# Low parts of the weights: a negated copy on ScalarE and an adding transfer in place of GpSimd's subtraction

## The chip, the cores and the metric

The kernel runs on one core of a Trainium2 chip. The metric is the device time of one execution in microseconds; the median of three runs of the kernel before is 2039.91 us (2033.06 to 2041.58).

## The reference

Two layers of a trunk, run for two groups of rows that share all weights: a prompt of 512 rows and a sample of 32 rows with cached state. One layer:

```
h = rmsnorm(x);  P = h @ w_in                      # 1024 -> 7688 columns, shared out to all branches
A: glu -> causal depthwise conv (31) -> LayerNorm -> silu -> @ w_conv_out
B: retention, 8 heads, rotary q/k, chunks -> GroupNorm * silu gate -> @ w_ret_out
C: forgetting attention, 8 heads, QK-norm, causal, cumulative log-forget bias -> @ w_fox_out
x = x + (sig(gA)*A + sig(gB)*B + sig(gC)*C) @ w_out
x = x + (gelu(causal dwconv3(h2 @ W_a)) * (h2 @ W_b)) @ W_down,   h2 = rmsnorm(x)
```

All inputs are fp32. The outputs are both groups' rows and their new states.

## The kernel before

Both groups are laid side by side as 544 columns (32 + 512), channels on the partitions. Every projection is a product of a weight block of 128 x 128 with the activations, in two halves of 272 columns. To come close to fp32 with fp32r matmuls, weights and activations are each split into a high part, which is the value rounded to fp32r, and a low part, which is value minus high part. One block takes three matmuls per half: high x high, high x low and low x high (`gemm`, L305).

The weights come in units of 8 blocks, a tile of 128 x 1024 (512 KB). There are 146 units per layer, 292 in all, packed in the order of use. The class `Stream` brings them in. `load_part` (L195) has SP issue the transfer of a unit into a `raw` tile, of which there are two. `split_part` has ScalarE write the high part into `hi` (L203), and then GpSimd subtract `hi` from `raw` into `lo` (L204). There are three `hi` and three `lo` buffers. The first two units are split on VectorE by the setup code (L415 to L421), the other 290 by `split`.

The order of work is the program's order, and every engine works its own queue in that order. Each projection is a `slot` (L311): it takes the next unit, then `ahead` splits the unit after the next and loads the one two further on, then a piece of side work runs (`tick`), then the gemm of 48 matmuls, then its eviction (`done`). So a unit's split is written down two gemms ahead of its use, and its `hi` waits until the gemm three units back has given up the buffer. GpSimd's other work is small or late: a few copies and memsets, the rotary products (L813, L815), two splits of the attention's keys and queries (L605, L609), partial sums of the convolution (L490).

Side work is woven between the gemms: the 31-tap convolution on VectorE (L483, 27 steps for each of four channel blocks and layer), the attention (L701 and L712 for the sample, L751 to L784 for the prompt, with exp and copies such as L765 on ScalarE), the retention (L858 to L920), the norms (rsqrt L343 to L353). R-scaled evictions are L394; in the FFN, L1138 to L1151 evict, convolve three taps and apply gelu. L444 evicts the first two gemms of all.

Of the kernel before, what the change touches and what calls it, by code (L numbers as in the profile page):

```python
# [11 lines left out]
F32 = mybir.dt.float32  # L12
F32R = mybir.dt.float32r
AF = mybir.ActivationFunctionType
ALU = mybir.AluOpType
# [96 lines left out]
def trunk(ctx, tc, x_in, wpack, wff, consts, params, s_conv, s_ret, s_cache, s_clf, s_ffn,  # L112
          y_out, o_conv, o_ret, o_fk, o_fv, o_lf, o_ffn):
    nc = tc.nc
    PS = bass.MemoryType.PSUM
    mm = nc.tensor.matmul
    act = nc.scalar.activation
    vtt = nc.vector.tensor_tensor
    stt = nc.vector.scalar_tensor_tensor
    gtt = nc.gpsimd.tensor_tensor  # L120
# [61 lines left out]
    class Stream:  # L182
# [14 lines left out]
        def split_part(self, u, i, sub, n=2):  # L197
            if i == 0:
                self.hl[u] = [upool.tile([P, UW], F32R, tag=t, name=t, bufs=3) for t in ("hi", "lo")]
                self.ns += 1  # L200
            hi, lo = self.hl[u]
            sl = slice(i * UW // n, (i + 1) * UW // n)
            act(hi[:, sl], self.raw[u][:, sl], AF.Copy)  # L203
            sub(lo[:, sl], self.raw[u][:, sl], hi[:, sl].bitcast(F32), op=ALU.subtract)  # L204
            if i == n - 1:
                self.raw.pop(u)

# [4 lines left out]
        def split(self, upto):  # L212
            while self.ns <= min(upto, DEPTH * NU - 1):
                self.load(self.ns)
                self.split_part(self.ns, 0, gtt, 1)

        def take(self):
            u = self.at
# [1078 lines left out]
```

## Time and profile before

| | us |
|---|---|
| median of 3 runs | 2039.91 |
| the profiled execution | 2039.84 |
| its span, first to last instruction | 2038.1 |
| TensorE busy | 1969.1 |
| VectorE busy | 1225.7 |
| GpSimd busy | 900.7 |
| ScalarE busy | 788.2 |
| transfers, mean share of the 16 engines | 29.2% |

PE is TensorE's matmul, PEld its weight load, DVE is VectorE, ACT is ScalarE, POOL is GpSimd and SP is SyncE, which issues all transfers here. L305 is line 305 of the kernel. Matmuls are pipelined: a duration of 0.29 us goes with a new matmul every 0.125 us. An arrow `<-` in brackets names what ended the idle time before an instruction. In the tables of stretches the columns are the bounds and the length of the stretch, the busy us of PE, PEld, DVE, ACT and POOL with their instructions in brackets, the granted TensorE clock as a share of 2.4 GHz, the busy share of the 16 transfer engines, and GB/s.

### The profile page before, as it was taken

Reading aid. Unit: us, or ns where it says so; the run is one execution under the profiler, and the core shown is the slowest. Engines: PE = TensorE matmul, PEld = TensorE weight load, DVE = VectorE, ACT = ScalarE, POOL = GpSimd, SP = SyncE. Lnnn points to the kernel's source line nnn. Section 1 sums busy time; section 2 is a strip of 40 time slices with the busy share of each in tenths; the row PEclk is TensorE's granted clock in tenths of the full one; section 3 lists DMA queues with packets and bytes.
Section 4 is the critical chain, followed back from the end, with each engine's and each line's share of the span. In section 5 each row is a group of like instructions: output and inputs, shape, how many; then the busy total and the mean of one; then the engine's idle time right before and its main releaser. Section 6 shows DMA issues by size and latency. Waiting matters only on the chain.

```text
span 2038.1 us, 37239 instructions
## 1 busy us (share of the span) xinstructions
PE 1969.1 (97%) x15768; PEld 1913.6 (94%) x15768; DVE 1225.7 (60%) x1641; ACT 788.2 (39%) x1172; POOL 900.7 (44%) x580
## 2 busy tenths in 40 slices
PE   8999998999999999999999888989999999999999
PEld 7987888999999999999999877889999999999999
DVE  5587989666355660466326979995653656505640
ACT  4354552264334331233335445523452343313331
POOL 4463544244444444444444645432444344444442
PEclk9999999999999999999999999999999999999999
DMA  5353312122232222222433622112223322222232
GB/s 200 92 174 108 94 48 76 58 73 87 90 127 90 87 89 89 86 91 87 131 112 105 182 85 88 53 56 67 81 83 101 120 83 85 93 83 94 83 105 76
DMA packets 69075, 194.22 MB, mean 95 GB/s; under 512 B 14012, under 2 KB 15660, under 8 KB 68524
## 3 DMA queue, kind: packets, MB, share of 16 engines
q1 hardware_dynamic: 68908, 191.84, 29.2%
q8 instruction: 124, 2.03, 0.4%
q14 instruction: 43, 0.35, 0.1%
HBM read 169.07 MB, written 9.89 MB: 88 GB/s over the span
## 4 chain that ended last, share of the span: by engine, by line
PE 71%; DVE 22%; ACT 3%; issue 3%; DMA 1%; POOL 0%; SPq 0%; DVEq 0%; ACTq 0%; POOLq 0%
PE acc L305 68%; DVE w L483 10%; DVE w L756 1%; DVE q L324 1%; ACT hi L203 1%; DVE w L755 1%; DVE w L394 1%; DVE mn L687 1%; DVE w L353 1%; PE s L752 0%; DVE w L352 0%; DVE q L843 0%; ACT q L323 0%; DVE w L873 0%; DVE q L1019 0%
## 5 line engine op out<-in xcount | busy, mean ns | idle before, releaser
L305 PE MATMUL acc<-q,hi 128*128 128x272 f32 x9344 | 1789.6, 291 | 23.3 <-ACT q L323 9.0
L305 PEld LDWEIGHTS acc<-q,hi 128*128 128x128 f32 x9344 | 1475.3, 189 | 42.8 <-issue 9.4
L305 PE MATMUL acc<-q,lo 128*128 128x272 f32 x4672 | 1349.6, 289 | 0.0
L204 POOL TENSOR_TENSOR lo<-raw,hi 128x1024 fp32r<-128x1024 f32 x290 | 714.4, 2464 | 849.4 <-ACT hi L203 811.6
L305 PEld LDWEIGHTS acc<-q,lo 128*128 128x128 f32 x4672 | 883.0, 189 | 0.0
L203 ACT ACTIVATE hi<-raw 128x1024 fp32r<-128x1024 f32 (+1 forms) x293 | 309.4, 1056 | 735.4 <-PE acc L305 601.7
L483 DVE SCALAR_TENSOR_TENSOR w<-w,par 128x574 f32<-128x574 f32 x208 | 247.4, 1190 | 3.5
L1179 DVE TENSOR_TENSOR q<-acc,q 128x544 f32<-128x544 f32 x32 | 23.2, 725 | 208.9 <-PE acc L305 208.9
L1146 DVE SCALAR_TENSOR_TENSOR w<-w,par 128x546 f32<-128x546 f32 x44 | 93.6, 2128 | 42.9 <-ACT w L1145 42.9
L394 DVE TENSOR_TENSOR w<-acc,R 128x544 f32<-128x544 f32 x78 | 56.1, 720 | 95.5 <-PE acc L305 95.4
L321 DVE TENSOR_TENSOR q<-w,q 128x544 fp32r<-128x544 f32 x44 | 92.4, 2099 | 31.9 <-ACT q L320 31.9
L1148 ACT ACTIVATE w<-w 128x546 f32<-128x546 f32 x44 | 29.1, 662 | 129.7 <-DVE w L1147 129.6
L689 ACT ACTIVATE w<-w,mn 128x128 f32<-128x128 f32 (+4 forms) x68 | 38.0, 559 | 81.4 <-DVE mn L687 79.1
L324 DVE SCALAR_TENSOR_TENSOR q<-q,par 128x544 fp32r<-128x544 f32 x24 | 49.0, 2042 | 22.4 <-ACT q L323 22.4
L1141 POOL COPY fb<-w 128x2 f32<-128x2 f32 x44 | 8.1, 185 | 117.8 <-DVE w L1138 117.8
L1138 DVE TENSOR_TENSOR w<-acc,R 128x32 f32<-128x32 f32 x44 | 8.4, 192 | 83.2 <-PE acc L305 83.0
L813 POOL TENSOR_TENSOR w<-w,cst 128x544 f32<-128x544 f32 x16 | 26.2, 1641 | 65.7 <-DMA w<-q 59.7
L692 ACT ACTIVATE w<-w,rs 128x128 f32<-128x128 f32 (+4 forms) x68 | 37.9, 557 | 32.1 <-DVE rs L691 31.7
L490 POOL TENSOR_TENSOR w<-w 128x574 f32<-128x574 f32 x24 | 43.4, 1809 | 12.8 <-ACT w L486 11.2
L330 DVE TENSOR_TENSOR wr<-w,wr 128x544 fp32r<-128x544 f32 x24 | 27.2, 1133 | 33.3 <-ACT wr L329 33.3
L352 DVE SCALAR_TENSOR_TENSOR w<-s,w 128x272 f32<-128x272 f32 (+1 forms) x60 | 23.7, 436 | 38.1 <-ACT w L349 38.1
L1018 DVE SCALAR_TENSOR_TENSOR w<-w,acc 128x544 f32<-128x544 f32 x32 | 23.0, 720 | 37.3 <-PE acc L305 37.0
(207 smaller groups left out, 1563.2 us busy)
## 6 DMA issues: line engine op xcount, KB each, us to landing
raw<-in_wpack_dram SPq DMA_DIRECT2D x291, 512.0 KB, 3.3
q<-wr SPq DMA_DIRECT2D x64, 128.0 KB, 2.4
w<-in_x_dram SPq DMA_DIRECT2D x16, 272.0 KB, 4.2
w<-q SPq DMA_DIRECT2D x64, 68.0 KB, 3.0
ck<-cscr SPq DMA_DIRECT2D x16, 256.0 KB, 3.4
out_dram<-wr SPq DMA_DIRECT2D x8, 272.0 KB, 2.4
out_dram<-w SPq DMA_DIRECT2D x8, 272.0 KB, 2.6
xn<-q SPq DMA_DIRECT2D x8, 272.0 KB, 4.0
```

The source lines that it names most:

```text
L203: act(hi[:, sl], self.raw[u][:, sl], AF.Copy)
L204: sub(lo[:, sl], self.raw[u][:, sl], hi[:, sl].bitcast(F32), op=ALU.subtract)
L305: mm(acc[:, h, :HN], w, half(x, h), start=(i == 0 and j == 0), stop=(i == n - 1 and j == len(passes) - 1))
L321: vtt(lo, src, hi.bitcast(F32), op=ALU.subtract)
L324: stt(lo, src, scale, hi.bitcast(F32), op0=ALU.mult, op1=ALU.subtract)
L394: vtt(two(out), acc, two(self.R), op=ALU.mult)
L483: stt(c, u[:, k : k + CO], pcol(w + k), c, op0=ALU.mult, op1=ALU.add)
L490: gtt(p, p, t, op=ALU.add)
L689: act(L[:, :n], L[:, :n], AF.Exp, scale=-1.0, bias=mn, accum_out=sm)
L692: act(L[:, :n], L[:, :n], AF.Copy, scale=rs)
L1146: stt(c, a[:, 1 : 1 + FO], pcol(w + 1), c, op0=ALU.mult, op1=ALU.add)
L1148: act(c, c, AF.Gelu)
```

## The change

For the 290 units that `split` prepares, `lo` is no longer computed by GpSimd. ScalarE writes the negative of `hi` into `lo`, and GpSimd issues a transfer from HBM that adds the unit's weights onto `lo`. The weights are thereby read from HBM twice, once into `raw` for `hi`, and once into the sum. The first two units keep VectorE's subtraction.

```diff
             hi, lo = self.hl[u]
             sl = slice(i * UW // n, (i + 1) * UW // n)
             act(hi[:, sl], self.raw[u][:, sl], AF.Copy)
-            sub(lo[:, sl], self.raw[u][:, sl], hi[:, sl].bitcast(F32), op=ALU.subtract)
+            if sub is None:
+
+                act(lo[:, sl], hi[:, sl].bitcast(F32), AF.Copy, scale=-1.0)
+                nc.gpsimd.dma_start(lo[:, sl], wpack[u][:, sl], accum_op=ALU.add)
+            else:
+                sub(lo[:, sl], self.raw[u][:, sl], hi[:, sl].bitcast(F32), op=ALU.subtract)
             if i == n - 1:
                 self.raw.pop(u)
...
         def split(self, upto):
             while self.ns <= min(upto, DEPTH * NU - 1):
                 self.load(self.ns)
-                self.split_part(self.ns, 0, gtt, 1)
+                self.split_part(self.ns, 0, None, 1)
```

## Rows read from the trace of the kernel before

**Rows 1.** The page: busy us (share of span) and instructions; chain shares by engine.
```profile
PE 1969.1 (97%) x15768; PEld 1913.6 (94%) x15768; DVE 1225.7 (60%) x1641; ACT 788.2 (39%) x1172; POOL 900.7 (44%) x580
...
PE 71%; DVE 22%; ACT 3%; issue 3%; DMA 1%; POOL 0%; SPq 0%; DVEq 0%; ACTq 0%; POOLq 0%
```

**Rows 2.** Table of stretches: from:to, length, busy us (instructions), clock, DMA share, GB/s.
```profile
102.00:408.00 306.00, 284.32 (x2344) 260.53 (x2344) 256.75 (x372) 135.18 (x263) 139.91 (x73) 0.97 0.30 93
408.00:1019.00 611.00, 607.86 (x4831) 605.98 (x4830) 313.78 (x376) 225.36 (x278) 269.95 (x193) 1.00 0.29 94
1121.00:1427.00 306.00, 281.18 (x2338) 256.44 (x2337) 255.73 (x361) 134.11 (x262) 136.56 (x69) 0.98 0.29 89
1427.00:1987.00 560.00, 556.86 (x4412) 554.98 (x4411) 292.62 (x349) 201.27 (x245) 248.16 (x182) 1.00 0.28 92
```

**Rows 3.** Table of waits, TensorE: us in total, times, longest us.
```profile
PE s L701 <- DVE w L712: 10.2, 2, 5.2
...
PE t L763 <- ACT w L765: 8.7, 7, 2.3
PE acc L305 <- DVE w L394: 8.5, 6, 2.5
PE s L631 <- DVE w L352: 7.3, 2, 3.7
...
PE o L892 <- DVE w L873: 5.2, 2, 2.6
```

**Rows 4.** Chain of waits, 102 to 200 us: start us, us, what.
```profile
159.57 0.83 DVE w L483
...
162.64 2.83 DVE w L483
```

**Rows 5.** Timeline, 155 to 171 us: start us, us, instruction, count [idle before <- releaser].
```profile
162.31 2.53 POOL L204 TENSOR_TENSOR lo<-raw,hi 128x1024 fp32r<-128x1024 f32 x1 [4.24 <-ACT hi L203]
...
169.98 1.07 PE L701 MATMUL s<-q,w 64*32 64x256 f32 x8 [4.98 <-DVE w L712]
```

**Rows 6.** Groups by line and shape: count | busy us, mean ns | idle before, releasers.
```profile
L204 POOL TENSOR_TENSOR lo<-raw,hi 128x1024 fp32r<-128x1024 f32 x290 | 714.4, 2464 | 849.4 <-ACT hi L203 811.6 <-DMA raw<-in_wpack_dram 20.7 <-PE t L763 14.8
L203 ACT ACTIVATE hi<-raw 128x1024 fp32r<-128x1024 f32 x291 | 308.2, 1059 | 735.0 <-PE acc L305 601.7 <-issue 122.8 <-DMA raw<-in_wpack_dram 6.3
L483 DVE SCALAR_TENSOR_TENSOR w<-w,par 128x574 f32<-128x574 f32 x208 | 247.4, 1190 | 3.5
L1146 DVE SCALAR_TENSOR_TENSOR w<-w,par 128x546 f32<-128x546 f32 x44 | 93.6, 2128 | 42.9 <-ACT w L1145 42.9
...
L1147 DVE SCALAR_TENSOR_TENSOR w<-w,par 128x546 f32<-128x546 f32 x44 | 34.7, 789 | 1.6
```

**Rows 7.** Table of stretches, L204 alone: DVE and POOL busy, clock, DMA share, GB/s.
```profile
102.00:408.00 306.00, 0.00 (x0) 83.12 (x33) 0.97 0.30 93
```

**Rows 8.** Timeline of a steady stretch in the FFN.
```profile
704.56 1.06 ACT L203 ACTIVATE hi<-raw 128x1024 fp32r<-128x1024 f32 x1 [4.03 <-PE acc L305]
...
705.70 2.40 POOL L204 TENSOR_TENSOR lo<-raw,hi 128x1024 fp32r<-128x1024 f32 x1 [0.62 <-ACT hi L203]
706.47 2.21 DVE L1146 SCALAR_TENSOR_TENSOR w<-w,par 128x546 f32<-128x546 f32 x1 [0.97 <-ACT w L1145]
...
716.59 1.06 ACT L203 ACTIVATE hi<-raw 128x1024 fp32r<-128x1024 f32 x1 [4.04 <-PE acc L305]
```

**Rows 9.** DMA issues: engine, operation, count, KB each, median us from issue to landing.
```profile
raw<-in_wpack_dram SPq DMA_DIRECT2D x291, 512.0 KB, 3.3
...
q<-in_s_cache_dram SPq DMA_DIRECT2D x2, 1024.0 KB, 7.0
```

**Rows 10.** Table of stretches, a steady one in the FFN's down projection.
```profile
764.30:815.20 50.90, 50.90 (x409) 50.90 (x408) 4.35 (x6) 9.54 (x9) 20.43 (x9) 1.00 0.27 89
```

**Rows 11.** Timeline of the start.
```profile
20.42 1.05 ACT L203 ACTIVATE hi<-raw 128x1024 fp32r<-128x1024 f32 x1
...
25.90 0.63 ACT L444 ACTIVATE w<-acc 128x544 f32<-128x544 f32 x1 [0.52 <-PE acc L305]
```

## The prediction

> **What bounds the kernel now.** The page's first part comes first: TensorE is busy in 97% of the span [rows 1]. A change that leaves the matmuls alone can win back only its idle time, 2038.1 - 1969.1 = 69.0 us. The table of stretches shows where that lies: 306.0 - 284.3 = 21.7 us in the first layer's attention and convolution part (102 to 408 us), 306.0 - 281.2 = 24.8 us in the second's (1121 to 1427), 3.1 us in each of the two long stretches with gates, FFN and down projection (408 to 1019, 1427 to 1987) [rows 2], and the other 16 us at the start, between the layers and at the end. So the two attention parts decide, with 46.5 us; I call them A and B. In them VectorE is busy 84% of the time (256.8 of 306), and the granted clock is 0.97 and 0.98 rather than 1.00: short times at the lower level (1.2 of 2.4 GHz), worth some 9 + 6 = 15 us.
>
> The table of waits names what TensorE idled for: 10.2 us for L712, 8.5 for L394, 7.3 for L352, 5.2 for L873, all on VectorE, 31 us together, and 8.7 us at 7 places for ScalarE's copy L765 [rows 3]; by their lines these belong to A and B. The chain of waits ahead of the longest one is a file of L483 convolution steps on VectorE: most take 0.83 us, some 2.83 [rows 4]. The timeline says which: the one of 2.83 us, at 162.64, runs beside GpSimd's subtraction L204 (162.31 to 164.84), and TensorE's 5 us of waiting at L701 end at the close of that file [rows 5].
>
> **What goes: the subtraction on GpSimd.** 290 instructions of 2464 ns, 714 us [rows 6]. GpSimd is not on the path (0% of the chain [rows 1]), so their own time is worth nothing. What counts is what they do to VectorE. L1146 and L1147 have the same form and 546 columns, yet take 2128 and 789 ns [rows 6]; L1146 is the one that falls beside L204 [rows 8]. L483 takes 1190 ns on average and 0.83 us when left alone [rows 4, 6]: 0.36 x 208 = 75 us too much; it is the convolution, which runs in A and B. GpSimd's own work in A is 139.9 us, of which L204 has 83.1, that is 59% [rows 2, 7]. I give the subtraction 59% of the 75: 45 us of VectorE's time released. L1146 would also shrink, by 1.3 us x 44, but it stands in the FFN, in the stretches where TensorE is busy 99% of the time [rows 2]: worth nothing.
>
> How much of the 45 us reaches the end? The 31 us of waits named for VectorE are the ceiling. In the file before L701 a stretched step costs 2.0 us of a 5.0 us wait [rows 4, 5]; other steps are stretched by GpSimd work that stays. Between none and all I take 60% of 31, by the 59%: **-19 us**. Fewer idle times leave fewer times at the lower clock: a quarter of 15, **-4 us**. Bounds: 0, and -31 - 15 = -46.
>
> **What comes: a second pass on ScalarE.** 290 x 1.06 us = 307 us [rows 6], 33 of them or 35 us in A [rows 7], on top of ScalarE's 135 of 306 [rows 2], so it becomes no bound. The new pass stands right behind `hi` in a queue that keeps its order, and what is queued behind it (tanh, exp, the copies L765, the splits) starts up to 1.06 us later. In the FFN that is covered: L1145 starts 1.06 us later, and the 2.2 us L1146 behind it should fall to about 0.8 [rows 6, 8]. In A and B, TensorE waits for L765 at 7 places [rows 3]; at most 7 x 1.06 = +7 us, at least 0, I take the middle, **+4 us**.
>
> **What comes: the adding transfer.** It waits for ScalarE's second pass, and GpSimd's copies, rotary products and klo splits queue behind it, as they queue today behind L204, which waits 812 us in all for `hi` [rows 6]. The matmuls now wait for its landing. The budget, from a steady part: `hi` runs from 704.56 to 705.62, when a gemm has just ended; its unit is used two gemms later, and the second one's end is seen at 716.59, 12.03 us on (6.0 us a gemm) [rows 8]. From the end of `hi` that is 10.9 us; less 1.06 for the second pass and 0.1 for the handover, 9.7 us are left for issue and landing. Today L204 ends at 708.10 [rows 8], with 8.4 us to spare.
>
> The trace has no transfer issued by GpSimd and none that adds, so both are bounded. Issue: between nothing and the 2.4 us of the arithmetic that it replaces; I take 1.0, nearer to the lower end since it works on no tile. Landing: a plain 512 KB weight load lands in 3.3 us, and 1024 KB, as much as target and source together, in 7.0 us [rows 9]. The engine time of a plain one: 0.27 of the 16 engines over 6.0 us [rows 10], 1.6 us. Adding must read the target too, so I take twice that, 3.2 us, and a landing of 3.3 + 1.6 + 0.6 = 5.5 us, between the two rows. Issue and landing make 6.5 us of 9.7: hidden in steady state. The engines would be at 0.27 x 3 = 0.81. The upper end for the adding is four times a plain load, 0.27 x 5 = 1.35, and that is not hidden (rival 2).
>
> The Trainium skill, in "Collectives: The Full Stack" (The bandwidth ceiling), says that a reducing transfer runs at half a copy's rate because it reads two sources, and not because the adder costs time. By it the 0.81 holds and the sum stands; no row here shows it.
>
> Not hidden is the start: unit 2's `hi` runs from 20.42 to 21.47, and its first gemm follows the one that L444 evicts at 25.90 [rows 11]. With 21.5 + 1.1 + 6.5 = 29.1 us the weights are about **+3 us** late, once; with the bounds 0 + 3.3 and 2.4 + 7.0 it is 0 to +6.
>
> **What moves.** The raw buffer comes free when `hi` ends, not when L204 ends, some 2.5 us sooner; SP, whose next weight load stands waiting for that buffer, gets on sooner, and with it the transfers queued behind. The next raw weights are early anyway (`hi` mostly waits for TensorE, 601.7 us [rows 6]), so I count it as 0.
>
> **The sum.** -19 - 4 + 4 + 3 = -16 us on the profiled execution's own 2039.84 us (span 2038.1), which is the median of the runs to 0.1 us: **2024 us**. Its bounds: -46 + 0 + 0 = -46 (1994) and 0 + 7 + 6 = +13 (2053); its own likely range is 1998 to 2035.
>
> **Rivals.** *1. No change, about 2037.* The issue holds VectorE up just as the subtraction did, for as long as it lasts, and A and B are paced by ScalarE. With 1.0 of 2.4 us held, 58% of the 19 us stay: -11 - 2 + 7 + 3 = -3 us. For it: the exp and tanh chains alternate between the two engines. Against: ScalarE is busy in only 44% of A. The Trainium skill, "SBUF — State Buffer" (Who interferes with whom), says that VectorE with two inputs in SBUF collides with GpSimd instructions that read SBUF, not with ones that only write. By that an issue would release VectorE entirely and this rival loses its first half; the rows show the collision with a reading instruction, none with a writing one. Chance 0.20.
>
> *2. Slower: the transfer engines become the bound.* It decides where adding costs three times a plain load's engine time: 0.27 x 4 = 1.08, and a gemm of 6.0 us waits for 6.5 us of transfers. In the two steady stretches, 611 + 560 = 1171 us [rows 2], 8% are 94 us: about 2135 us. At four times, 1.35, it is +410 us: 2450. Landing over 8.7 us behind a 1.0 us issue does the same by latency: TensorE waits in every unit. For it: each of 290 weight tiles passes, and 27% is used already. Against: reading HBM and reading SBUF are both plain work, and twice leaves 19% free. Chance 0.25.
>
> *3. Slightly slower, about 2053.* The upper bounds +7 and +6 with no relief on VectorE, because GpSimd's rotary and klo work, which stays, meets the convolution as often as L204 did. Chance 0.05.
>
> **From this to the numbers.** Forecast 0.50, rivals 0.20, 0.25, 0.05. A difference of 0.5% (10 us) is about what a measurement can tell from none. Faster 0.50 (forecast), same 0.20 (rival 1), slower 0.30 (rivals 2 and 3). About 0.05 lie under 1998, and 0.15 above 2140 (rival 2 beyond threefold cost), so the range is 1998 to 2140; rival 2 sets its upper end.
>
> **What would show it.** Right: L483 near 0.9 to 1.0 us on average and L1146 near 0.8; TensorE's idle time in A and B down from 46 to about 25 us; no wait of L305 for a transfer into `lo` after unit 3; a transfer share near 0.8 in the FFN. Wrong: waits of L305 for `lo` in every unit, a transfer share at 1.0, a landing over 8.7 us (rival 2); L483 still at 1.1 us or more (rival 1); more waits for L765 and later `hi` (rivals 1 and 3).

## The result: 2007 us, 1.5% faster, twice the forecast's gain

The kernel after takes 2006.89 us (median, 2003.81 to 2014.27) where the kernel before took 2039.67: a ratio of 0.9847 [0.9829, 0.9865], 32.8 us less. The forecast was 16 us less. The profiled execution took 2007.52 us, its span is 2005.8. Line numbers behind the diff are 5 higher than before: L305 is now L310, L483 is L488, L1146 is L1151.

The page of the kernel after: busy time by engine, then the DMA queues (GpSimd's is q0), then the chain's shares.

```profile
PE 1964.9 (98%) x15768; PEld 1911.1 (95%) x15768; DVE 943.4 (47%) x1641; ACT 1065.2 (53%) x1462; POOL 425.9 (21%) x580
...
q0 software_dynamic: 41760, 152.06, 45.2%
q1 hardware_dynamic: 68908, 191.84, 29.5%
...
PE 38%; DVE 2%; ACT 2%; DMA 1%; issue 1%; SPq 0%; DVEq 0%; ACTq 0%
```

TensorE's idle time is 2005.8 - 1964.9 = 40.9 us where it was 69.0 [rows 1]: 28.1 us less. Its busy time fell by 4.2 us although it does the same 15768 matmuls; less of it runs at the lower clock (the granted clock of the span is 0.992 where it was 0.991). The two make the 32.3 us of the span. VectorE does the same 1641 instructions in 943 us where it took 1226, 23% less. The chain's shares of the two pages can't be set side by side: the chain of the kernel after is followed back only to 1122 us, and its shares add up to 44%. From 1122 us to the end, VectorE has 42 of the chain's 883 us, where before it has 207 of 916; transfers have 22 where they had 3.

The table of stretches says where. Its columns are those of [rows 2], and its times are fixed from the start, so that each part of the work now lies some microseconds off.

```profile
102.00:408.00 306.00, 295.94 (x2462) 271.21 (x2462) 226.49 (x384) 177.60 (x313) 86.14 (x76) 0.99 0.67 157
408.00:1019.00 611.00, 608.80 (x4829) 607.16 (x4828) 219.12 (x372) 318.50 (x374) 111.27 (x193) 1.00 0.80 181
1121.00:1427.00 306.00, 299.63 (x2508) 276.73 (x2507) 223.43 (x384) 184.22 (x315) 81.62 (x71) 0.99 0.65 153
1427.00:1987.00 560.00, 558.20 (x4425) 556.57 (x4424) 188.88 (x324) 273.97 (x316) 102.74 (x183) 1.00 0.79 179
```

A's idle time fell from 21.7 to 10.1 us and B's from 24.8 to 6.4, together from 46.5 to 16.4, with the clock from 0.97 and 0.98 to 0.99. In the first FFN stretch VectorE shed 30% of its time (313.78 to 219.12), and TensorE gained 0.9 us there and 1.3 in the second. ScalarE, with the new pass, works 178 us of A instead of 135, and in the FFN it has become the busier of the two, 318.50 against 219.12.

TensorE's waits (us in total, times, longest), first a line of before that [rows 3] leave out, then the kernel after:

```profile
PE acc L305 <- ACT q L323: 9.0, 3, 6.1
```

```profile
PE acc L310 <- ACT q L328: 7.8, 3, 6.3
PE acc L310 <- DMA lo<-in_wpack_dram: 6.2, 2, 5.8
PE s L636 <- DVE w L357: 5.7, 2, 2.8
...
PE s L756 <- DVE w L760: 2.4, 1, 2.4
PE o L743 <- ACT w L728: 1.8, 2, 1.0
...
PE s L706 <- DVE w L717: 1.3, 1, 1.3
...
PE acc L310 <- DVE w L399: 0.4, 1, 0.4
PE o L786 <- ACT w L770: 0.2, 1, 0.2
```

Three of the four largest waits of before are gone but for a rest [rows 3]: L712 (now L717) from 10.2 to 1.3, L394 (now L399) from 8.5 to 0.4, and ScalarE's L765 (now L770) from 8.7 at 7 places to 0.2. The fourth, for L323 (now L328), is 7.8 where it was 9.0. The largest new name is the landing of `lo`, at two places and not 290; L760 (2.4) and L728 (1.8) are new too. How the idle time is shared out among the names differs from kernel to kernel: in the two below that differ from this one only in their first units, the wait for L717 is 8.9 and 6.3 us again.

Groups by line and shape, then a steady piece of the FFN's timeline:

```profile
L206 ACT ACTIVATE lo<-hi 128x1024 fp32r<-128x1024 f32 x290 | 305.2, 1052 | 4.6
...
L207 POOL DMA_DIRECT2D lo<-in_wpack_dram x290 | 251.6, 868 | 1263.6 <-ACT lo L206 1205.0 <-issue 17.5 <-DVE w L488 13.5
...
L488 DVE SCALAR_TENSOR_TENSOR w<-w,par 128x574 f32<-128x574 f32 x208 | 195.7, 941 | 3.6
...
L1151 DVE SCALAR_TENSOR_TENSOR w<-w,par 128x546 f32<-128x546 f32 x44 | 34.7, 788 | 83.5 <-ACT w L1150 83.5
```

```profile
697.18 1.06 ACT L206 ACTIVATE lo<-hi 128x1024 fp32r<-128x1024 f32 x1
...
698.54 0.86 POOL L207 DMA_DIRECT2D lo<-in_wpack_dram  x1 [1.22 <-ACT lo L206]
...
699.01 0.79 DVE L1151 SCALAR_TENSOR_TENSOR w<-w,par 128x546 f32<-128x546 f32 x1 [1.94 <-ACT w L1150]
```

L1151 starts at 699.01, while GpSimd is still issuing (698.54 to 699.40), and takes its 0.79 us. Beside the subtraction the same step took 2.21 [rows 8]; over all 44 the mean fell from 2128 to 788 ns [rows 6]. L488 fell from 1190 to 941 ns and not to the 0.83 us of a step left alone [rows 4]; GpSimd's own convolution and rotary arithmetic stayed, and the last experiment shows what they hold back.

The transfers' landings (KB each, median us from the start of the issue), the start of the timeline, where the wait for `lo` stands, and the landing of the transfer issued at 23.45:

```profile
raw<-in_wpack_dram SPq DMA_DIRECT2D x291, 512.0 KB, 3.5
lo<-in_wpack_dram POOLq DMA_DIRECT2D x290, 512.0 KB, 5.5
```

```profile
22.09 1.05 ACT L206 ACTIVATE lo<-hi 128x1024 fp32r<-128x1024 f32 x1
...
23.45 1.01 POOL L207 DMA_DIRECT2D lo<-in_wpack_dram  x1 [6.32 <-ACT lo L206]
...
32.45 0.60 PE L310 MATMUL acc<-q,lo 128*128 128x272 f32 x1 [5.75 <-DMA lo<-in_wpack_dram]
```

```profile
DMA to landing us min/median/max: 9.0/9.0/9.0
```

A landing is counted from the start of the issue, and so holds the issue's own time: 23.45 + 9.0 = 32.45, where TensorE goes on. In the steady state 5.5 us, 0.87 of them the issue, fit the 9.7 us of the budget. At the start, where the engines also bring in the other inputs, the unit issued at 23.45 holds TensorE up for 5.75 us at 32.45.

### The profile page after: what moved, and what is told of

Same layout as the page of the kernel before. It is cut to its first block, busy times and chain, and to the rows that moved or that the text cites. A ratio compares the mean times of both kernels' runs of the same rounds, so it can differ in the third digit from the quotient of the medians.

```text
span 2005.8 us, 37801 instructions
## 1 busy us (share of the span) xinstructions
PE 1964.9 (98%) x15768; PEld 1911.1 (95%) x15768; DVE 943.4 (47%) x1641; ACT 1065.2 (53%) x1462; POOL 425.9 (21%) x580
## 3 DMA queue, kind: packets, MB, share of 16 engines
q0 software_dynamic: 41760, 152.06, 45.2%
## 5 line engine op out<-in xcount | busy, mean ns | idle before, releaser
L310 PE MATMUL acc<-q,hi 128*128 128x272 f32 x9344 | 1787.1, 290 | 13.9 <-ACT q L328 7.8
L310 PEld LDWEIGHTS acc<-q,hi 128*128 128x128 f32 x9344 | 1473.8, 189 | 31.1 <-ACT q L328 8.8
L310 PE MATMUL acc<-q,lo 128*128 128x272 f32 x4672 | 1350.1, 289 | 6.2 <-DMA lo<-in_wpack_dram 6.2
L310 PEld LDWEIGHTS acc<-q,lo 128*128 128x128 f32 x4672 | 882.2, 189 | 6.9 <-DMA lo<-in_wpack_dram 6.9
L203 ACT ACTIVATE hi<-raw 128x1024 fp32r<-128x1024 f32 (+1 forms) x293 | 309.6, 1057 | 642.9 <-PE acc L310 640.7
L207 POOL DMA_DIRECT2D lo<-in_wpack_dram x290 | 251.6, 868 | 1263.6 <-ACT lo L206 1205.0
L206 ACT ACTIVATE lo<-hi 128x1024 fp32r<-128x1024 f32 x290 | 305.2, 1052 | 4.6
L488 DVE SCALAR_TENSOR_TENSOR w<-w,par 128x574 f32<-128x574 f32 x208 | 195.7, 941 | 3.6
L399 DVE TENSOR_TENSOR w<-acc,R 128x544 f32<-128x544 f32 x78 | 56.1, 720 | 117.8 <-PE acc L310 117.5
L1151 DVE SCALAR_TENSOR_TENSOR w<-w,par 128x546 f32<-128x546 f32 x44 | 34.7, 788 | 83.5 <-ACT w L1150 83.5
L326 DVE TENSOR_TENSOR q<-w,q 128x544 fp32r<-128x544 f32 x44 | 31.9, 725 | 33.7 <-ACT q L325 33.7
L770 ACT ACTIVATE w<-t 128x128 f32<-128x128 f32 (+3 forms) x64 | 27.4, 428 | 34.1 <-PE t L768 32.2
L760 DVE SCALAR_TENSOR_TENSOR w<-ck,CM,s 128x128 f32<-128x128 f32 (+3 forms) x64 | 34.5, 539 | 17.8 <-PE s L757 17.8
L335 DVE TENSOR_TENSOR wr<-w,wr 128x544 fp32r<-128x544 f32 x24 | 21.8, 907 | 41.0 <-ACT wr L334 41.0
```

The costliest lines, as they stand in the source:

```text
L206: act(lo[:, sl], hi[:, sl].bitcast(F32), AF.Copy, scale=-1.0)
L207: nc.gpsimd.dma_start(lo[:, sl], wpack[u][:, sl], accum_op=ALU.add)
L310: mm(acc[:, h, :HN], w, half(x, h), start=(i == 0 and j == 0), stop=(i == n - 1 and j == len(passes) - 1))
L326: vtt(lo, src, hi.bitcast(F32), op=ALU.subtract)
L399: vtt(two(out), acc, two(self.R), op=ALU.mult)
L488: stt(c, u[:, k : k + CO], pcol(w + k), c, op0=ALU.mult, op1=ALU.add)
```

## The experiments

Each is built from the kernel after unless the text says otherwise. The ratio is to the kernel before on the same chip, with a 95% interval; a difference between two experiments is worked out from their ratios times 2040 us.

### The lock put back: reading against writing

The first experiment keeps the adding transfer and has GpSimd subtract again, into the raw tile, whose content nobody uses any more.

```diff
     act(lo[:, sl], hi[:, sl].bitcast(F32), AF.Copy, scale=-1.0)
+    gtt(self.raw[u], self.raw[u], hi.bitcast(F32), op=ALU.subtract)
     nc.gpsimd.dma_start(lo[:, sl], wpack[u][:, sl], accum_op=ALU.add)
```

> The changed kernel, with the old subtraction issued on GpSimd once more per unit, into the raw tile that is no longer needed, ahead of the adding transfer; its result is not used. It brings back the 2.4 us of GpSimd with two inputs in SBUF, GpSimd's full queue and the late release of the raw buffer. If the gain came from VectorE no longer being held by the subtraction: L483's step back near 1.15 to 1.2 us, TensorE idle near 45 us in the two attention parts, time 2033 to 2048 us. If the gain came from somewhere else (the release of the raw tile alone, a different order of transfers), the theories part in the next run, not in this one; if neither matters, it stays near 2007.

Measured: 2110.37 us, 1.0363 [1.0346, 1.0379]. The direction held and the size did not: the time went far past that of before. The second one occupies GpSimd in the same place, for 1.9 us instead of 2.5, with two fills that read no tile.

```diff
+    nc.gpsimd.memset(self.raw[u], 0.0)
+    nc.gpsimd.memset(self.raw[u], 1.0)
     nc.gpsimd.dma_start(lo[:, sl], wpack[u][:, sl], accum_op=ALU.add)
```

> As the run before, but in place of the subtraction two memsets of the raw tile, about 1.1 us each: GpSimd is as busy, the raw tile comes free as late, but nothing on GpSimd reads SBUF. If VectorE is held only by a GpSimd instruction that reads: L483's step stays near 0.94 us and the time near 2007 us (2000 to 2015). If GpSimd's occupied queue and the late raw tile made the old kernel slow: 2033 to 2048 us.

Measured: 2029.37 us, 0.9964 [0.9951, 0.9977]. Groups by line of the kernel that subtracts again, with its stretch A:

```profile
L207 POOL TENSOR_TENSOR raw<-raw,hi 128x1024 f32<-128x1024 f32 x290 | 717.6, 2474 | 704.8 <-issue 573.7 <-ACT hi L203 88.2 <-POOL fb L1147 27.4
...
L489 DVE SCALAR_TENSOR_TENSOR w<-w,par 128x574 f32<-128x574 f32 x208 | 251.0, 1207 | 3.6
```

```profile
102.00:408.00 306.00, 275.54 (x2171) 249.12 (x2171) 259.86 (x361) 159.96 (x291) 162.92 (x106) 0.95 0.61 142
```

And of the kernel that fills:

```profile
L208 POOL MEMSET raw<- 128x1024 f32 x290 | 276.9, 955 | 12.9
...
L490 DVE SCALAR_TENSOR_TENSOR w<-w,par 128x574 f32<-128x574 f32 x208 | 202.0, 971 | 3.7
```

```profile
102.00:408.00 306.00, 291.49 (x2394) 265.46 (x2393) 224.64 (x377) 170.23 (x303) 147.81 (x143) 0.98 0.65 154
```

GpSimd is busy 163 us of A with the subtraction and 148 with the fills, but the convolution step takes 1207 ns on average in the one kernel and 971 in the other, and TensorE idles 30.5 us of A against 14.5. Between the two kernels lie 81 us, and they have the transfer's lateness in common: `lo` lands 7.0 us after its issue in both, and TensorE waits for it at 4 places in both, 9.3 and 9.2 us. So VectorE is held by a GpSimd instruction that reads two tiles, and hardly by one that only writes (941 ns in the kernel after, which has neither). The Trainium skill says the same in "SBUF — State Buffer" (Who interferes with whom); here it has its number. The fills cost 24 us over the kernel after all the same. The landing is 1.5 us longer and the issue stands behind 1.9 us of filling, but 1.9 + 7.0 = 8.9 us still fit the budget of 9.7, and the steady state loses next to nothing: from the start of ScalarE's pass L203 on unit 48 to its start on unit 161 it is 698.3 us, where the kernel after has 697.3. The loss is in A and B: from unit 15 to 48, which holds A, it is 303.2 us instead of 295.3, and from unit 161 to 194, which holds B, 302.4 instead of 289.7. What queues behind the fills or behind the longer landing there was not separated.

That the subtraction put back costs 105 us over the kernel after, when the whole change had brought 31, points to a pass and an adding transfer that had eaten a part of what the relief brought. The following runs price them.

### The change in parts of the program

Units 15 to 47 of each layer's weights are those split during A and B. One kernel makes the change for these 66 units alone, the next for the other 224:

```diff
-    self.split_part(self.ns, 0, None, 1)
+    self.split_part(self.ns, 0, None if 15 <= self.ns % NU < 48 else gtt, 1)
```

> The adding transfer for units 15 to 47 of each layer alone (the attention and convolution parts A and B, 66 units); the other 224 keep GpSimd's subtraction. If the whole gain is made in A and B, and the first unit's late low part costs 6 to 7 us at the start: 2000 us (1995 to 2006), with a transfer share near 0.3 in the FFN. If part of the gain comes from the FFN or from the other stretches: 2010 to 2025 us.

> The reverse: the adding transfer for all units but 15 to 47 of each layer. If A and B hold the whole gain and the start costs 6 to 7 us: 2044 us (2038 to 2050), no faster than the kernel before. If the gain is spread: 2015 to 2030 us.

Measured: 2005.3 us, 0.984 [0.9822, 0.9857], for A and B alone; 2039.35, 1.0008 [0.9998, 1.0019], for the rest. Their sum, -33 and +2 us, is the whole change's -31. The first kernel's FFN stretch, and the second's convolution and FFN steps:

```profile
408.00:1019.00 611.00, 607.19 (x4807) 605.15 (x4808) 307.76 (x368) 222.43 (x272) 269.62 (x192) 1.00 0.28 96
```

```profile
L488 DVE SCALAR_TENSOR_TENSOR w<-w,par 128x574 f32<-128x574 f32 x208 | 248.1, 1193 | 3.5
...
L1151 DVE SCALAR_TENSOR_TENSOR w<-w,par 128x546 f32<-128x546 f32 x44 | 34.7, 789 | 83.5 <-ACT w L1150 83.5
```

In the second kernel L1151 is down to 789 ns and the convolution is still at 1193; on balance nothing is won. The +2 is a balance: from the pass L203 on unit 2 to that on unit 15 it takes 87.0 us where the kernel before takes 81.8, with the late `lo` of the start, and it makes up about as much over units 48 to 161 and 194 to 291 (699.1 to 696.3 and 594.9 to 592.9). In the first kernel VectorE works 308 us of the FFN stretch instead of 219, and TensorE idles 3.8 us of it instead of 2.2. An engine's time is worth what the stage makes of it.

### The price of ScalarE's pass, of the addition and of the relief

This one is the kernel before with the pass added ahead of its subtraction, which then overwrites the result:

```diff
     act(hi[:, sl], self.raw[u][:, sl], AF.Copy)
+    if n == 1 and u > 1:
+        act(lo[:, sl], hi[:, sl].bitcast(F32), AF.Copy, scale=-1.0)
     sub(lo[:, sl], self.raw[u][:, sl], hi[:, sl].bitcast(F32), op=ALU.subtract)
```

> The kernel before, with ScalarE's negated pass written into lo and then overwritten by GpSimd's subtraction: the price of 290 x 1.06 us on ScalarE by itself, with VectorE as slow as before. By the prediction +4 us (0 to +7), 2040 to 2047 us. By the trace of the changed kernel, where the waits for L765 fell from 8.7 to 0.2 us although ScalarE had this pass: no more than 0 to +3. If ScalarE's queue were what paces A and B: +15 us and more.

Measured: 2061.61 us, 1.0121 [1.0098, 1.0144], 25 us more than before: the theory by which ScalarE's queue paces A and B (15 us and more) had it, the other two did not. From the pass L203 on unit 15 to that on unit 48 it is 318.7 us instead of 309.6, from unit 161 to 194 318.7 instead of 310.2. Next, the kernel after without the pass and without the addition, its `lo` loaded from HBM as it is, so that the low parts hold the weights:

```diff
-    act(lo[:, sl], hi[:, sl].bitcast(F32), AF.Copy, scale=-1.0)
-    nc.gpsimd.dma_start(lo[:, sl], wpack[u][:, sl], accum_op=ALU.add)
+    nc.gpsimd.dma_start(lo[:, sl], wpack[u][:, sl])
```

> ScalarE's negated pass is left out, and GpSimd's transfer writes the weights plainly into lo instead of adding (lo is then not the low part). VectorE stays released, and both the pass of 1.05 us and half of the transfer's engine time are gone. If the price of the pass (+23 us when it was put alone into the kernel before) is still paid in the changed kernel: 1980 to 1990 us. If the pass costs little once VectorE is released, since TensorE then has few idle times left in A and B (16 us): 1996 to 2004 us, of which 4 to 6 are the start.

Measured: 1972.3 us, 0.9671 [0.9658, 0.9683], under both ranges. Last, the pass kept and only the addition left out, with the same content of `lo`:

```diff
-    nc.gpsimd.dma_start(lo[:, sl], wpack[u][:, sl], accum_op=ALU.add)
+    nc.gpsimd.dma_start(lo[:, sl], wpack[u][:, sl])
```

> The changed kernel with a plain transfer in place of the adding one, behind ScalarE's pass as before (lo is overwritten and is not the low part). Leaving out the pass and the adding together brought 34 us. If ScalarE's pass is what costs that: this run keeps the pass, and stays at 2000 to 2007 us. If the adding's second reading of the tile, its longer landing (5.5 against 4.0 us) and the fuller transfer engines cost it: 1972 to 1982 us.

Measured: 1989.84 us, 0.9759 [0.9739, 0.9779], between the two ranges. Stretch A and GpSimd's issues, first of the kernel with neither pass nor addition, then of the kernel with the pass, with its queue of GpSimd's transfers and TensorE's wait for them:

```profile
102.00:408.00 306.00, 302.60 (x2568) 280.70 (x2567) 230.04 (x395) 153.40 (x287) 73.47 (x75) 1.00 0.52 162
```

```profile
L206 POOL DMA_DIRECT2D lo<-in_wpack_dram x290 | 155.6, 537 | 1480.6 <-PE acc L309 1403.1 <-PE s L341 35.9 <-PE t L767 16.2
```

```profile
102.00:408.00 306.00, 299.33 (x2518) 275.57 (x2517) 228.00 (x393) 182.14 (x320) 75.93 (x77) 1.00 0.54 160
```

```profile
q0 software_dynamic: 41760, 152.06, 26.3%
```

```profile
PE acc L310 <- DMA lo<-in_wpack_dram: 4.4, 1, 4.4
```

The steps from one kernel to the next take the change apart. TensorE's idle and busy time are those of each page (span less busy, and busy):

| kernel | TensorE idle, us | TensorE busy, us | ratio | step, us |
|---|---|---|---|---|
| before | 69.0 | 1969.1 | 1 | |
| subtraction gone, plain load | 22.5 | 1947.8 | 0.9671 | -67 |
| and the pass on ScalarE | 32.4 | 1955.7 | 0.9759 | +18 |
| and the load adds (after) | 40.9 | 1964.9 | 0.9847 | +18 |

Each step has an interval of some 3 to 5 us to either side. All of them move idle time and busy time together: the matmuls are the same, and the granted clocks of the four spans are 0.991, 1.000, 0.996 and 0.992, so the busy time that comes and goes is put down to the clock. The relief takes 46.5 us of idle time, and 21.3 us of clock go with it. The two kernels in the middle also have other content in `lo` (the weights, not the low parts); that this moves the clock was not tested, but at the start, up to 102 us, it is 0.95 with either content.

The start of ScalarE's pass L203 on one and the same unit tells where each step falls (us; units 15 to 48 hold A, 161 to 194 hold B):

| kernel | unit 2 | unit 15 | unit 48 | unit 161 | unit 194 | unit 291 |
|---|---|---|---|---|---|---|
| before | 20.42 | 102.25 | 411.81 | 1110.93 | 1421.12 | 2016.05 |
| subtraction gone, plain load | 20.91 | 99.48 | 381.61 | 1074.29 | 1358.39 | 1947.86 |
| and the pass on ScalarE | 21.48 | 105.97 | 394.35 | 1088.73 | 1374.46 | 1965.55 |
| and the load adds (after) | 21.00 | 107.79 | 403.09 | 1100.35 | 1390.00 | 1983.24 |

The whole change loses 5.0 us up to unit 15 and wins 14.3 in A and 20.5 in B. The relief is worth 27.4 us in A and 26.1 in B. Of the 18 us of the pass, 5.9 are lost up to unit 15, where the load now waits for the pass and TensorE waits 4.4 us for its landing, which it does nowhere in the kernel without the pass; 6.3 are lost in A and 1.6 in B. The adding costs 6.9 us in A and 3.9 in B. These are single executions, and two kernels that are the same in A, the kernel after and the one whose change starts at unit 8, differ by 5.0 us there.

### Where the adding transfer would stop hiding

A plain load of the same tile into a buffer in HBM that nobody reads is added to each of the loads on SP's queue:

```diff
     dma(self.raw[u][:, sl], wpack[u][:, sl])
+    if n == 1:
+        dma(dpool.tile([P, UW], F32, tag="twin", name="twin", bufs=4), wpack[u][:, sl])
```

> The changed kernel, and with every weight load of a unit a third reading of it by a plain transfer from HBM to a buffer in HBM that nobody reads: the transfer engines get about 0.27 more, 0.80 + 0.27 = 1.07 in the steady stretches. If a share of 1.0 of the transfer engines' time is where they become the bound: the steady stretches grow by 7%, about +80 us, 2075 to 2110 us, with TensorE waiting for lo and ScalarE for raw. If the share is only an average that leaves room (queues of several transfers in flight): under 2025 us.

Measured: 2093.65 us, 1.0273 [1.0249, 1.0298]. It was not the even load that was meant: the added loads waited for no reader, ran ahead and were all issued in the first half. The stretch 408 to 1019, TensorE's wait over the whole run, and the landings in that stretch:

```profile
408.00:1019.00 611.00, 554.45 (x4204) 544.23 (x4205) 197.47 (x338) 280.84 (x330) 97.07 (x172) 0.97 0.98 314
```

```profile
PE acc L312 <- DMA lo<-in_wpack_dram: 63.7, 44, 6.2
```

```profile
lo<-in_wpack_dram POOLq DMA_DIRECT2D x87, 512.0 KB, 10.9
```

The repair writes `hi` out to HBM, which can't run ahead of the pass that makes it:

```diff
     act(lo[:, sl], hi[:, sl].bitcast(F32), AF.Copy, scale=-1.0)
+    dma(dpool.tile([P, UW], F32R, tag="twin", name="twin", bufs=4).bitcast(F32), hi.bitcast(F32))
     nc.gpsimd.dma_start(lo[:, sl], wpack[u][:, sl], accum_op=ALU.add)
```

> The changed kernel, and for every unit one more plain transfer of 512 KB, from hi to a buffer in HBM that nobody reads, which can't run ahead since it waits for hi (in the earlier run the third reading ran far ahead of its unit and doubled the load for half of the time). Planned share in the steady stretches 0.80 + 0.27 = 1.07. If the share of the transfer engines' time is the bound: about 6.4 to 6.6 us a gemm there, +80 us over 1171 us, 2075 to 2105 us, TensorE waiting for lo in most units. If a transfer of this direction costs the engines less or shares their time with the adding: under 2030 us.

Measured: 2022.77 us, 0.9914 [0.9901, 0.9927]. The same three views:

```profile
408.00:1019.00 611.00, 608.76 (x4839) 606.91 (x4838) 221.45 (x376) 321.37 (x378) 110.82 (x193) 1.00 0.98 265
```

```profile
PE acc L311 <- DMA lo<-in_wpack_dram: 14.1, 9, 6.5
```

```profile
lo<-in_wpack_dram POOLq DMA_DIRECT2D x101, 512.0 KB, 7.5
```

Both kernels have the engines busy 98% of this stretch. In the one TensorE idles 56.6 us of it, in the other 2.2, as in the kernel after, although by rival 2's sum the repaired kernel's engines stand at 0.80 + 0.27 = 1.07. What tells the two apart is the landing: 7.5 us fit the 9.7 of the budget, 10.9 do not. What the written copy of `hi` takes of the engines by itself was not measured, so the 1.07 is a plan and not a reading. The 14 us that the repaired kernel loses against the kernel after lie outside this stretch: 8 us in the waits for `lo`, 9 places instead of 2, and 9.7 us of B idle instead of 6.4.

### The start, and one step further

The change left out for the first four units, then for the first eight:

```diff
-    self.split_part(self.ns, 0, None, 1)
+    self.split_part(self.ns, 0, gtt if self.ns < 4 else None, 1)
```

> The changed kernel, with GpSimd's subtraction kept for units 2 and 3, so that the first adding transfer is needed later. The late low part of unit 2 costs 5.8 us of waiting in the changed kernel; if that wait is all there is to it: 2000 us (1997 to 2004), -6 to -7. If the next unit is late in its place: 2003 to 2008.

> The changed kernel with GpSimd's subtraction kept for units 2 to 7 (with 2 and 3 alone, unit 4 was still 1.9 us late). If the start is only a matter of the first units: 1999 to 2003 us, without any wait for lo. If later units are late in their place: 2003 to 2007 us.

Measured: 2002.75 us, 0.9829 [0.9807, 0.9852], and 2001.4 us, 0.9812 [0.9793, 0.9831]. The wait for `lo` falls from 6.2 us to 1.9 and to 0.4. The second has the lowest ratio of the kernels that leave nothing out, 7 us under the kernel after and 3.5 under the first; its interval overlaps theirs, so their order isn't shown. The last experiment hands two more of GpSimd's additions, one of the convolution and one of the rotary part, to adding transfers:

```diff
-    gtt(p, p, t, op=ALU.add)
+    nc.gpsimd.dma_start(p, t, accum_op=ALU.add)
...
-    gtt(q, q, w, op=ALU.add)
+    nc.gpsimd.dma_start(q, w, accum_op=ALU.add)
```

> As the run before, and two more GpSimd additions become adding transfers, from SBUF to SBUF: the partial sums of the convolution (L490 before, 24) and the second rotary step (L815 before, 16). What still holds VectorE in A and B is GpSimd's own arithmetic: there L483's step takes 0.96 us, 0.14 above the free one, and one 128-column L756 took 3.16 us beside two such instructions, ahead of a 2.4 us wait of TensorE. If the lock by reading instructions is the cause throughout: step near 0.87, 3 to 10 us faster than the run before, 1990 to 1999 us. If it's not the reading but something else in A and B: no change or slower by the longer way of the sums.

Measured: 2025.06 us, 0.9935 [0.9916, 0.9954], 25 us slower than the kernel from the eighth unit that it is built on. Groups by line, then waits of GpSimd and of TensorE:

```profile
L488 DVE SCALAR_TENSOR_TENSOR w<-w,par 128x574 f32<-128x574 f32 x208 | 174.7, 840 | 3.6
...
L495 POOL DMA_DIRECT2D w<-w x24 | 20.8, 865 | 79.2 <-DMA w<-w 41.2 <-issue 16.7 <-ACT w L491 8.2
```

```profile
POOL w L495 <- DMA w<-w: 41.2, 9, 7.1
```

```profile
PE t L867 <- DVE st L914: 9.1, 2, 4.8
...
PE acc L310 <- DMA lo<-in_wpack_dram: 7.4, 3, 3.3
```

VectorE's step came down to the 0.84 us of one left alone, so the lock is gone altogether, and the kernel is slower. Each addition of the convolution builds on the one before, and GpSimd stands still up to 7.1 us until that has landed, with the issues of `lo` queued behind. TensorE's waits for `lo` came back at 3 places, and a wait of 9.1 us at L867 where there was 1.3. That these two make up the 25 us isn't shown.

## Why the prediction was right in sign and half the size

**The mechanism held.** GpSimd's subtraction holds VectorE while it reads, an issue does not, and the gain is made in A and B: shown by the two kernels that occupy GpSimd, 81 us apart, and by the two that split the change, -33 and +2. Rival 1's first half (the issue holds VectorE) falls with L1151's 788 ns; its second, that ScalarE paces A and B, has something to it, as the price of the pass shows.

**The term that failed is the relief: -19 and -4, measured -67.** The step was "The 31 us of waits named for VectorE are the ceiling", of which 60% was taken. A wait has the name of whoever came last. In the kernel without subtraction, pass and addition, A and B idle 3.4 and 2.2 us instead of 46.5 together, so the relief is 41 us and not 19, and the waits named for ScalarE's L765, 8.7 us before, go too (0.2 there), which suggests that ScalarE was late because VectorE had been. The -67 is the subtraction against a plain load: what the load and the earlier release of the raw buffer add to it or take from it is in it too. The 45 us of released time were sized well (249 ns off each of 208 L488 steps, 52 us), but I then discounted them. The busy share said otherwise: VectorE was busy 84% of A, and it had 22% of the chain. The clock gave 21.3 us, not 4: I took a quarter of 15 us, while in that kernel nearly all of it went with the idle time (granted clock 1.000).

**The pass on ScalarE: +4, bounded at +7, measured +18** (+25 in the kernel before). The bound counted the 7 places where TensorE waited for L765 and gave each one pass. But A and B alternate between VectorE and ScalarE; that a pass of 1.05 us standing in ScalarE's queue delays every step of a chain that needs ScalarE, also those whose end is named for VectorE, is argued from that and from the waits spread over many names. Shown is the price, and that 5.9 of the 18 us are the start, where the load stands behind the pass. ScalarE's busy share in A, 44% before, did not say it.

**The adding transfer in steady state: 0, measured +18 with the start.** The numbers were close: issue 0.87 (1.0 taken), share 0.80 (0.81), landing 5.5, and no wait for `lo` in the steady FFN. The prediction set 6.5 us against the budget, issue and landing together; the landings of [rows 9] that it built on already hold an issue, and so do the measured 5.5, which stand alone against the 9.7. Yet a plain load in its place, issued in 0.54 us and landing in 4.3, is 18 us faster. TensorE's idle time grows by 8.5 us between the two: 2.2 at the start, 3.4 in A, 0.6 in B, the rest in the other stretches. Which of the two (the longer issue in GpSimd's queue, or the engines' added work) makes it in A isn't shown.

**The start: +3, bounds 0 to +6.** The waits there are 6.2 us, just past the upper bound; leaving the change out for four or eight units brings 4 and 7 us, with intervals of 5 to 6 to either side. The landing at the start is what was missed: 9.0 us for the first and 7.1 for the median of the first six, where 6.5 were taken with the issue. The engines' share doesn't explain it, 0.78 there and 0.80 in the FFN with its 5.5; the cause stays open.

**Rival 2 was priced by the wrong quantity.** It let the loss begin where the sum of the engines' shares passes 1.0. At a sum of 1.07 the share read 0.98 and the FFN lost nothing; at the same 0.98, with a landing of 10.9 us, it lost 54 us. Its second condition, a landing over 8.7 us (9.7 with the issue counted once), is the one that parts these two runs, and the kernel after stays clear of it by 3.2 us (4.2). The Trainium skill's rule in "Collectives: The Full Stack" (The bandwidth ceiling), told there of collectives, is that a reducing transfer runs at half a copy's rate. This case comes near it: q0 takes 45.2% of the engines when adding and 26.3% when not, for the same 152 MB, which is 1.7 times and not twice, and the FFN's share of 0.80 is where the prediction put it with twice, 0.81.

**Earlier raw buffers: 0.** It wasn't tried by itself. SP's weight loads still stand waiting, 1495 us in all, now for `hi` instead of `lo`, and the landing of a raw load is 3.5 us where it was 3.3 [rows 9].

The forecast lay 17 us above the time because -23 should have been -67, and +7 should have been +36. Errors of 44 and 29 us with opposite signs left one of 15 by the ratios, 17 by the medians. The sum came out near the time for the wrong sizes.

## What to carry to other kernels

To find out whether two engines hold each other up, compare one form of instruction with itself, beside another engine's work and alone (2128 against 789 ns here), and then ask what the other engine's instruction reads. When such a hold goes from a stage where two engines take turns, count all of the stage's idle time and the clock that follows it as within reach, not only the waits that bear one engine's name; and count an added pass on the partner engine in the same way. In these runs a transfer was hidden as long as its landing, counted from the start of the issue, fitted the time from its trigger to its use; the busy share of the transfer engines was not that limit, and for first units with less time ahead of them the old path is the safer one (the wait for `lo` falls from 6.2 to 0.4 us; that the kernel is faster by it isn't shown).

## What was not expected of the hardware

- An adding transfer of 512 KB from HBM onto a tile, issued by GpSimd: 0.87 us to issue and 5.5 us from the start of the issue to the landing, against 0.54 and 4.3 us for a plain one on the same queue.
- Transfer engines busy 98% of an FFN stretch, at 265 GB/s, without any loss there to matmuls that wait for these very transfers (2.2 us of idle time, as in the kernel after).
- A ScalarE pass of 1.05 us, 290 times, on an engine busy 39% of the span, costs 18 to 25 us (in the kernel of the 18, 5.9 of them at the start).
- GpSimd doing arithmetic on two tiles 2.5 us per unit costs 105 us where the same engine's 1.9 us of fills cost 24.
